# First feed-forward pairs: five k-tiles in two halves and three whole, where all eight were halved, and the lower half's squares summed on VectorE

## The chip, the cores and the metric

One core of a Trainium2 chip runs the whole kernel. The metric is the device time of one execution in microseconds (us). TensorE does the matrix products, VectorE and ScalarE the elementwise work, GpSimd a few additions, SyncE issues the transfers.

## The reference

One layer of an encoder for 512 positions and 1024 channels, in float32. This case concerns the seam between its mixing part and its feed-forward part (`rms_norm` divides each position's row by its root mean square):

```python
h = h + rms_norm(merged @ w_out[i], g_mix_post[i])

hn = rms_norm(h, g_ffn_pre[i])
f_gate, f_up = jnp.split(hn @ w_ffn_in[i], 2, axis=-1)
f = (jax.nn.silu(f_gate) * f_up) @ w_ffn_out[i]
h = h + rms_norm(f, g_ffn_post[i])
```

`w_ffn_in` has 1024 rows and 2 x 2816 columns, so the hidden size is 22 tiles of 128.

## The kernel before

Channels lie on the 128 partitions and positions along the free axis, so an activation of 1024 channels is eight tiles ("k-tiles") of 128 x 512. The positions are also taken in two halves of 256, `lo_half` and `hi_half`. For precision each product is made of three matmuls (`mm3`): both operands are split into a high and a low part, and high x high, high x low and low x high are accumulated in one PSUM bank. Splitting is a cast on ScalarE and a subtraction on VectorE.

`Residual.tile(k)` makes one k-tile of the new `h` for one half: VectorE multiplies the mixed output `o_all` by the inverse root mean square `o_inv` and adds it to `h_all`, ScalarE writes the scaled high part `hg[k][:, 0]`, and VectorE, one step later (`flush`), the low part `hg[k][:, 1]`. The feed-forward product uses `hg`, that is `h` with its gain but without its own root mean square; that factor, `h_inv`, is multiplied in afterwards, in `swiglu`, position by position. It needs the sum of squares of all eight tiles, `h_sums`: ScalarE squares (`square_h`), and `add_h` adds up. `inv_rms` then sums over partitions with a matmul into `ps_stat` and runs `rsqrt`, eight dependent VectorE instructions.

The first three gate and up pairs of the feed-forward product (six banks, six weight blocks) are made with the k-tile in the outer loop (`product_k_outer`), so that TensorE can start as soon as the first k-tiles of the lower half are there: `STAT_A` = 2 k-tiles of the lower half come ahead of the matmul for `o_inv` of the upper half, the other six behind it, and then the upper half's eight, with the matmul for `h_inv` ahead of the last one (`STAT_H` = 7). The lower half's squares are added on GpSimd, the upper half's on VectorE between the residual's steps. Inside `with order():` every engine keeps the order in which the code is written. There are 7 PSUM banks for such products: six are held by the three pairs, the seventh takes `ffn_tile(0)`, and `ffn_tile(1)` needs the first bank that `swiglu` has read.

Of the kernel before, what the change touches and what calls it, by code (L numbers as in the profile page):

```python
# [20 lines left out]
KT = D // P  # L21
# [10 lines left out]
FULL = slice(0, T)  # L32
# [18 lines left out]

DMA_K = 5
STAT_K, STAT_A, STAT_H, STAT_F = 3, 2, 7, 2
MIX_CUT = ((), (0,), (1, 2), (3, 4, 5, 6, 7))
PLE_CUT = (1, 2, 3, 4, 5, 6, 8)
PLE_SPLIT = 3
# [29 lines left out]
def hybrid_block(  # L86
# [7 lines left out]
    nc = tc.nc  # L94
    order = InOrder(tc)
    dve, act_e, pe = order.engine(nc.vector), order.engine(nc.scalar), order.engine(nc.tensor)
# [9 lines left out]
    def bank(name):  # L106
        return psum.tile([P, T], F32, tag="ps", name=name)

    def wide_tile(name):
        return wide.tile([P, KT, T], F32, tag="wide", name=name)  # L110

    def slot(tag, name, dt=F32R, shape=(2, T)):
        return act.tile([P, *shape], dt, tag=tag, name=name, bufs=6 if tag == "tm" else 8)

    def t2(name, n=T):
        return tmp.tile([P, n], F32, tag="t2", name=name)

    def row(name):
        return stat.tile([P, T], F32, tag="row", name=name)
# [99 lines left out]
    def mm3(out, wh, wl, xh, xl, first, last):  # L219
        pe.matmul(out, lhsT=wh, rhs=xh, start=first, stop=False)  # L220
        pe.matmul(out, lhsT=wh, rhs=xl, start=False, stop=False)
        pe.matmul(out, lhsT=wl, rhs=xh, start=False, stop=last)

    def blk(w, k):
        return w[:, k * P:(k + 1) * P]
# [5 lines left out]
            mm3(ps[:, hs], blk(hi, i), blk(lo, i), a[:, 0, hs], a[:, 1, hs],  # L231
                k0 + i == 0, last and i == len(acts) - 1)

    def product_k_outer(banks, blocks, acts, hs, ks=range(KT)):
        for k in ks:
            a = acts[k]
            for ps, (hi, lo) in zip(banks, blocks):
                mm3(ps[:, hs], blk(hi, k), blk(lo, k), a[:, 0, hs], a[:, 1, hs],
                    k == 0, k == len(acts) - 1)


    background = []
# [29 lines left out]
    def inv_rms(sums, y):  # L272

        rsqrt(y, channel_mean(sums), t2("rs_t", sums.shape[1]))
# [13 lines left out]
    def add_sq(sums, sq, i, engine):  # L288
        if i == 1:
            dve.scalar_tensor_tensor(out=sums, in0=sq, scalar=EPS * D / P, in1=sums,  # L290
                                     op0=ALU.add, op1=ALU.add)
        else:
            engine.tensor_tensor(out=sums, in0=sums, in1=sq, op=ALU.add)
# [134 lines left out]
    banks = [bank("ps_first") for _ in range(2 * N_RAW)]  # L428
# [310 lines left out]
    o_all = wide_tile("o_all")  # L739
# [26 lines left out]
    hg = [slot("cv", f"hg{k}") for k in range(KT)]  # L766
    o_sums = row("o_sums")
    h_sums = row("h_sums")
    h_inv = row("h_inv")

    def mix_tile(n, w, hs):
        ps = bank("ps_o")
        product(ps, w, mix_T, hs)
        act_e.activation(out=o_all[:, n, hs], in_=ps[:, hs], func=AF.Copy, scale=col("g_mix_post", n))
        if n == 0:
            act_e.activation(out=o_sums[:, hs], in_=ps[:, hs], func=AF.Square)
            return None
        return square(ps[:, hs], "o_sq")

    def add_mixed(sq, n, hs):  # L780
        if n:
            add_sq(o_sums[:, hs], sq, n, dve)
# [4 lines left out]
    def square_h(k, hs):  # L787
        sq = o_all[:, k, hs] if k else h_sums[:, hs]
        act_e.activation(out=sq, in_=h_all[:, k, hs], func=AF.Square)

    def add_h(k, hs, engine):
        if k:
            add_sq(h_sums[:, hs], o_all[:, k, hs], k, engine)

    lo_half, hi_half = HALVES
    with order():
        for n in range(KT - N_HALF):
            sq = mix_tile(n, weights.get(2), FULL)
            add_mixed(sq, n, FULL)
            weights.ahead((5, 7, 9, 10)[n])  # L800
        late = [weights.get(0) for _ in range(N_HALF)]
        blocks = [weights.get(0) for _ in range(2 * N_PAIR)]
        for i in range(N_HALF):
            n = KT - N_HALF + i
            add_mixed(mix_tile(n, late[i], lo_half), n, lo_half)
        sqs = []
        for i in range(N_HALF):
            n = KT - N_HALF + i
            sq = mix_tile(n, late[i], hi_half)
            if i == 0:  # L810
                y = t2("o_inv", H)
                inv_rms(o_sums[:, lo_half], y)
                res = Residual(o_all, lo_half, y, hg, ffn_gain)
            sqs.append((sq, n))
            for k in MIX_CUT[i]:
                res.tile(k)
                if sqs:
                    add_mixed(*sqs.pop(0), hi_half)
        res.flush()


        banks = [bank("ps_f") for _ in range(2 * N_PAIR)]
        product_k_outer(banks, blocks, hg, lo_half, range(STAT_A))
        for k in range(KT):
            square_h(k, lo_half)
            add_h(k, lo_half, nc.gpsimd)
        y = t2("o_inv", H)
        inv_rms(o_sums[:, hi_half], y)
        res = Residual(o_all, hi_half, y, hg, ffn_gain)
        for k in range(KT):  # L830
            res.tile(k)
            if k > 1:
                add_h(k - 2, hi_half, dve)
            if k:
                square_h(k - 1, hi_half)
        res.flush()
        square_h(KT - 1, hi_half)
        add_h(KT - 2, hi_half, dve)
        add_h(KT - 1, hi_half, dve)
        weights.ahead(2)  # L840
        product_k_outer(banks, blocks, hg, lo_half, range(STAT_A, KT))
        product_k_outer(banks, blocks, hg, hi_half, range(STAT_H))
        inv_rms(h_sums, h_inv)
        product_k_outer(banks, blocks, hg, hi_half, range(STAT_H, KT))

    f_T = []

# [67 lines left out]
    with order():  # L915
# [29 lines left out]
        blocks = [weights.get(0) for _ in range(2)]  # L945
        k = 0
# [9 lines left out]
        banks = [bank("ps_pg") for _ in range(N_LAST)]  # L956
# [82 lines left out]
```

## Time and profile before

| | |
|---|---|
| median of 3 runs | 981.67 us (981.36 to 981.8) |
| the profiled execution's own time | 981.52 us |
| its span, first to last instruction | 979.7 us |
| TensorE busy | 972.2 us (99%) |
| VectorE / ScalarE / GpSimd busy | 672.3 / 350.2 / 83.3 us |
| mean granted TensorE clock | 0.999 |

The profiled execution takes 1.82 us more than its span, and its time is 0.15 us below the median. A busy TensorE is one that always has a matmul under way. How fast they follow one another is read from the starts of successive ones, since they overlap.

### The profile page before, as it was taken

To read this page: it belongs to the slowest core of one execution; us is meant where nothing else is said; L and a number is where in the kernel's file an instruction comes from. 1 tells how busy PE (TensorE), PEld (TensorE's weight loads), DVE (VectorE), ACT (ScalarE), POOL (GpSimd) and SP (SyncE) were. 2 spreads that over 40 slices of the span, in tenths; PEclk is the share of its full clock that TensorE was granted. 3 is DMA by queue.
4 is the path that set the end of the run, shared out by engine and by line. 5 is a ranking of instruction groups with operands and counts; after the bars stand their busy time and mean duration, and the time that the engine had idled before them with its cause. 6 is when DMAs were issued, how large, how long until landed. Compare 5 with 4: busy or idle time off the path is not lost.

```text
span 979.7 us, 11730 instructions
## 1 busy us (share of the span) xinstructions
PE 972.2 (99%) x4683; PEld 818.0 (83%) x4683; DVE 672.3 (69%) x905; ACT 350.2 (36%) x487; POOL 83.3 (9%) x63
## 2 busy tenths in 40 slices
PE   9999999999999999999999999999999999999998
PEld 6888888788888878888888998888888888888897
DVE  6987789999988899967555677544454432223575
ACT  7522323432214432246326433323232322223442
POOL 1100013000013702260000010000000000000000
PEclk9999999999999999999999999999999999999999
DMA  8723322223222322332337112232323233334312
GB/s 305 192 95 100 113 90 73 100 86 101 94 86 91 104 86 89 105 108 86 108 111 274 46 44 79 94 103 90 108 86 104 88 99 98 99 86 139 110 42 86
DMA packets 30726, 102.76 MB, mean 105 GB/s; under 512 B 3536, under 2 KB 4048, under 8 KB 30672
## 3 DMA queue, kind: packets, MB, share of 16 engines
q1 hardware_dynamic: 29808, 99.75, 31.1%
q0 software_dynamic: 720, 2.23, 1.3%
q8 instruction: 36, 0.59, 0.2%
q14 instruction: 18, 0.15, 0.0%
q10 hardware_dynamic: 144, 0.04, 0.0%
HBM read 97.68 MB, written 2.10 MB: 102 GB/s over the span
## 4 chain that ended last, share of the span: by engine, by line
PE 94%; DVE 4%; issue 1%; ACT 0%; DMA 0%; SPq 0%; ACTq 0%
PE ps_f L73 25%; PE ps_br L73 13%; PE ps_fo L73 12%; PE ps_gate L73 12%; PE ps_nat L73 6%; PE ps_ag L73 6%; PE ps_pg L73 5%; PE ps_o L73 5%; PE ps_z L73 4%; PE ps_first L73 3%; DVE lo L73 1%; PE ps_ple L73 1%; PE ps_pool L73 1%; DVE v_all L73 1%; DVE acc L73 1%
## 5 line engine op out<-in xcount | busy, mean ns | idle before, releaser
L73 ACT CAST hi<-raw 128x1024 fp32r<-128x1024 f32 (+1 forms) x157 | 161.6, 1031 | 454.0 <-PE ps_br L73 88.4
L73 DVE TENSOR_TENSOR lo<-raw,hi 128x1024 fp32r<-128x1024 f32 (+2 forms) x155 | 203.9, 1317 | 107.1 <-ACT hi L73 106.6
L73 DVE SCALAR_TENSOR_TENSOR acc<-h_conv,vec,acc 128x511 f32<-128x511 f32 (+14 forms) x240 | 183.3, 764 | 5.2
L73 PE MATMUL ps_f<-hg,hi 128*128 128x512 f32 (+1 forms) x624 | 184.4, 378 | 0.0
L73 PEld LDWEIGHTS ps_f<-hg,hi 128*128 128x128 f32 x624 | 115.1, 188 | 21.7
L73 PE MATMUL ps_gate<-hn,hi 128*128 128x512 f32 x384 | 119.5, 392 | 0.9 <-DVE gated L73 0.9
L73 PE MATMUL ps_f<-hg,lo 128*128 128x512 f32 (+1 forms) x312 | 117.8, 378 | 0.0
L73 PE MATMUL ps_fo<-f,hi 128*128 128x512 f32 (+1 forms) x396 | 110.8, 366 | 0.0
L73 PEld LDWEIGHTS ps_gate<-hn,hi 128*128 128x128 f32 x384 | 71.9, 188 | 17.1 <-DVE gated L73 1.3
L73 PEld LDWEIGHTS ps_fo<-f,hi 128*128 128x128 f32 x396 | 71.7, 189 | 12.1
L73 PE MATMUL ps_nat<-hi,hn 128*128 128x512 f32 x256 | 78.8, 389 | 0.0
L73 PE MATMUL ps_gate<-hn,lo 128*128 128x512 f32 x192 | 74.8, 390 | 0.0
L73 PE MATMUL ps_fo<-f,lo 128*128 128x512 f32 (+1 forms) x198 | 72.4, 365 | 0.0
L73 PEld LDWEIGHTS ps_f<-hg,lo 128*128 128x128 f32 x312 | 58.7, 188 | 11.0
L73 PEld LDWEIGHTS ps_nat<-hi,hn 128*128 128x128 f32 x256 | 48.1, 188 | 10.0
L73 DVE TENSOR_TENSOR f<-ps_f,h_inv 128x512 f32<-128x512 f32 x22 | 15.2, 689 | 56.5 <-PE ps_f L73 56.5
L73 PE MATMUL ps_nat<-lo,hn 128*128 128x512 f32 x128 | 49.8, 389 | 0.0
L73 PE MATMUL ps_ag<-hn,hi 128*128 128x512 f32 x160 | 49.3, 389 | 0.0
L73 PEld LDWEIGHTS ps_fo<-f,lo 128*128 128x128 f32 x198 | 37.3, 189 | 6.1
L73 PEld LDWEIGHTS ps_gate<-hn,lo 128*128 128x128 f32 x192 | 36.0, 188 | 7.5
L73 DVE TENSOR_TENSOR silu<-ps_f,h_inv 128x512 f32<-128x512 f32 x22 | 15.2, 690 | 36.3 <-PE ps_f L73 36.2
L73 PE MATMUL ps_br<-pool,hi 128*128 128x512 f32 x128 | 39.6, 389 | 0.0
(221 smaller groups left out, 1560.2 us busy)
## 6 DMA issues: line engine op xcount, KB each, us to landing
raw<-in_w_mix SPq DMA_DIRECT2D x90, 512.0 KB, 3.3
raw<-in_w_ffn_in SPq DMA_DIRECT2D x44, 512.0 KB, 3.3
raw<-in_w_ffn_out SPq DMA_DIRECT2D x16, 448.0 KB, 3.3
raw<-in_w_ffn_out SPq DMA_DIRECT2D x8, 512.0 KB, 3.6
raw<-in_w_ple_gate SPq DMA_DIRECT2D x8, 512.0 KB, 3.8
x_all<-in_xT SPq DMA_DIRECT2D x8, 256.0 KB, 6.4
h_all<-in_xT SPq DMA_DIRECT2D x4, 512.0 KB, 6.2
out_dram<-pg SPq DMA_DIRECT2D x7, 256.0 KB, 2.0
```

Source lines behind the costliest of these rows:

```text
L73: inst = op(*args, **kw)
```

## The change

In the block that makes the first three pairs, three things differ. The lower half's squares are no longer added on GpSimd as they are made, but on VectorE behind the upper half's. `K_HALF` = 5 k-tiles are still multiplied in halves, the other three at the full width of 512 positions. And since the lower half has started each bank, the upper half's first matmul doesn't clear it (`started`).

```diff
+K_HALF = 5
...
-    def product_k_outer(banks, blocks, acts, hs, ks=range(KT)):
+    def product_k_outer(banks, blocks, acts, hs, ks=range(KT), started=False):
...
-                    k == 0, k == len(acts) - 1)
+                    k == 0 and not started, k == len(acts) - 1)
...
-    def add_h(k, hs, engine):
+    def add_h(k, hs):
         if k:
-            add_sq(h_sums[:, hs], o_all[:, k, hs], k, engine)
+            add_sq(h_sums[:, hs], o_all[:, k, hs], k, dve)
...
         for k in range(KT):
             square_h(k, lo_half)
-            add_h(k, lo_half, nc.gpsimd)
...
         square_h(KT - 1, hi_half)
-        add_h(KT - 2, hi_half, dve)
-        add_h(KT - 1, hi_half, dve)
+        add_h(KT - 2, hi_half)
+        add_h(KT - 1, hi_half)
+        for k in range(KT):
+            add_h(k, lo_half)
         weights.ahead(2)
-        product_k_outer(banks, blocks, hg, lo_half, range(STAT_A, KT))
-        product_k_outer(banks, blocks, hg, hi_half, range(STAT_H))
+        product_k_outer(banks, blocks, hg, lo_half, range(STAT_A, K_HALF))
+
+        product_k_outer(banks, blocks, hg, hi_half, range(K_HALF), started=True)
+        product_k_outer(banks, blocks, hg, FULL, range(K_HALF, STAT_H))
         inv_rms(h_sums, h_inv)
-        product_k_outer(banks, blocks, hg, hi_half, range(STAT_H, KT))
+        product_k_outer(banks, blocks, hg, FULL, range(STAT_H, KT))
```

On TensorE, this is the end of the lower half's k-tile 4 (`hg4`) and what follows it; `ps_f` with a number is a bank, `x2` two matmuls with the same weights. Before:

```order
L73 MATMUL ps_f_4321<-hg4_3847,hi_4036 128x256 x2
L73 MATMUL ps_f_4321<-hg4_3847,lo_4037 128x256
L73 MATMUL ps_f_4316<-hg5_3848,w_hi_3948 128x256 x2
L73 MATMUL ps_f_4316<-hg5_3848,w_lo_3949 128x256
L73 MATMUL ps_f_4317<-hg5_3848,w_hi_3983 128x256 x2
```

The same place in the changed kernel:

```order
L75 MATMUL ps_f_4321<-hg4_3847,hi_4036 128x256 x2
L75 MATMUL ps_f_4321<-hg4_3847,lo_4037 128x256
L75 MATMUL ps_f_4316<-hg0_3843,w_hi_3948 128x256 x2
L75 MATMUL ps_f_4316<-hg0_3843,w_lo_3949 128x256
L75 MATMUL ps_f_4317<-hg0_3843,w_hi_3983 128x256 x2
```

Behind the lower half's k-tile 4 came the lower half's k-tiles 5 to 7; now the upper half's k-tile 0 (`hg0`) comes at once, three k-tiles of half width sooner.

On VectorE, this is the end of the lower half's residual, the `rsqrt` for the upper half's `o_inv`, and the first upper tile (`hg_3843` is k-tile 0, `hg_3850` k-tile 7). Before:

```order
L73 SCALAR_TENSOR_TENSOR hg_3850<-h_all,vec,hg_3850 128x256
L73 SCALAR_TENSOR_TENSOR h_sums<-o_all,h_sums 128x256
L73 TENSOR_SCALAR o_inv<-ps_stat 128x256
...
L73 SCALAR_TENSOR_TENSOR o_inv<-rs_t,o_inv 128x256
L73 TENSOR_TENSOR o_all<-o_all,o_inv 128x256
L73 TENSOR_TENSOR h_all<-h_all,o_all 128x256
L73 TENSOR_TENSOR o_all<-o_all,o_inv 128x256
L73 SCALAR_TENSOR_TENSOR hg_3843<-h_all,vec,hg_3843 128x256
```

In the changed kernel:

```order
L75 SCALAR_TENSOR_TENSOR hg_3850<-h_all,vec,hg_3850 128x256
L75 TENSOR_SCALAR o_inv<-ps_stat 128x256
...
L75 SCALAR_TENSOR_TENSOR o_inv<-rs_t,o_inv 128x256
L75 TENSOR_TENSOR o_all<-o_all,o_inv 128x256
L75 TENSOR_TENSOR h_all<-h_all,o_all 128x256
L75 TENSOR_TENSOR o_all<-o_all,o_inv 128x256
L75 SCALAR_TENSOR_TENSOR hg_3843<-h_all,vec,hg_3843 128x256
```

One addition of squares is gone from between the lower half's last tile and the `rsqrt`; the rest of that chain is as it was.

The last place is VectorE behind the upper half's last tile, ahead of the split of the next two weight blocks (`w_lo`) and of `h_inv`. Before:

```order
L73 SCALAR_TENSOR_TENSOR hg_3850<-h_all,vec,hg_3850 128x256
L73 TENSOR_TENSOR h_sums<-h_sums,o_all 128x256 x2
L73 TENSOR_TENSOR w_lo<-raw,w_hi 128x1024 x2
L73 TENSOR_SCALAR h_inv<-ps_stat 128x512
L73 TENSOR_TENSOR rs_t<-h_inv 128x512
```

In the changed kernel:

```order
L75 SCALAR_TENSOR_TENSOR hg_3850<-h_all,vec,hg_3850 128x256
L75 TENSOR_TENSOR h_sums<-h_sums,o_all 128x256 x2
L75 SCALAR_TENSOR_TENSOR h_sums<-o_all,h_sums 128x256
L75 TENSOR_TENSOR h_sums<-h_sums,o_all 128x256 x6
L75 TENSOR_TENSOR w_lo<-raw,w_hi 128x1024 x2
L75 TENSOR_SCALAR h_inv<-ps_stat 128x512
```

Seven additions now stand between the upper half's sums and the split of the weights.

## Rows read from the trace of the kernel before

**Rows 1.** The page: busy time, share of the span, instructions.

```profile
PE 972.2 (99%) x4683; PEld 818.0 (83%) x4683; DVE 672.3 (69%) x905; ACT 350.2 (36%) x487; POOL 83.3 (9%) x63
```

**Rows 2.** TensorE's waits: for whom, us in total, times, longest.

```profile
PE ps_gate L73 <- DVE gated L73: 0.9, 1, 0.9
```

**Rows 3.** Timeline of TensorE: start, us, operation, count.

```profile
566.23 0.40 PE L73 MATMUL ps_f<-hg,w_hi 128*128 128x256 f32 x2
...
572.71 0.40 PE L73 MATMUL ps_f<-hg,w_hi 128*128 128x256 f32 x2
...
587.83 1.02 PE L73 MATMUL ps_stat<-h_sums,mean_mat 128*128 128x512 f32 x2
...
590.84 0.63 PE L73 MATMUL ps_f<-hg,w_hi 128*128 128x512 f32 x2
...
596.31 0.62 PE L73 MATMUL ps_f<-hg,w_hi 128*128 128x512 f32 x2
...
601.75 0.62 PE L73 MATMUL ps_f<-hg,w_hi 128*128 128x512 f32 x2
```

**Rows 4.** Timeline of VectorE, upper half's `rsqrt` and first tiles.

```profile
562.26 0.48 DVE L73 SCALAR_TENSOR_TENSOR hg<-h_all,vec,hg 128x256 fp32r<-128x256 f32 x1 [0.58 <-ACT hg L73]
...
563.22 0.42 DVE L73 TENSOR_SCALAR o_inv<-ps_stat 128x256 int32<-128x256 int32 x1
563.67 0.82 DVE L73 TENSOR_TENSOR rs_t<-o_inv 128x256 f32<-128x256 f32 x1
...
566.32 0.42 DVE L73 TENSOR_TENSOR rs_t<-rs_t,ps_stat 128x256 f32<-128x256 f32 x1
...
568.99 0.42 DVE L73 TENSOR_TENSOR h_all<-h_all,o_all 128x256 f32<-128x256 f32 x1
...
569.99 0.48 DVE L73 SCALAR_TENSOR_TENSOR hg<-h_all,vec,hg 128x256 fp32r<-128x256 f32 x1 [0.24 <-ACT hg L73]
570.39 0.42 DVE L73 TENSOR_TENSOR h_all<-h_all,o_all 128x256 f32<-128x256 f32 x1
...
571.39 0.48 DVE L73 SCALAR_TENSOR_TENSOR hg<-h_all,vec,hg 128x256 fp32r<-128x256 f32 x1 [0.24 <-ACT hg L73]
```

**Rows 5.** Timeline of GpSimd in the same stretch.

```profile
563.47 2.53 POOL L293 TENSOR_TENSOR h_sums<-h_sums,o_all 128x256 f32<-128x256 f32 x3 [124.82 <-ACT o_all L73]
...
566.08 2.60 POOL L293 TENSOR_TENSOR h_sums<-h_sums,o_all 128x256 f32<-128x256 f32 x3
```

**Rows 6.** Timeline of VectorE, the same chain for the lower half.

```profile
546.58 0.42 DVE L73 TENSOR_SCALAR o_inv<-ps_stat 128x256 int32<-128x256 int32 x1 [2.10 <-PE ps_stat L73]
...
550.71 0.42 DVE L73 TENSOR_TENSOR h_all<-h_all,o_all 128x256 f32<-128x256 f32 x1
```

**Rows 7.** Timeline of TensorE where it resumes after a wait.

```profile
185.72 0.73 PE L73 MATMUL ps_gate<-hn,hi 128*128 128x512 f32 x2 [0.87 <-DVE gated L73]
186.29 0.40 PE L73 MATMUL ps_gate<-hn,lo 128*128 128x512 f32 x1
```

**Rows 8.** Timeline of VectorE behind the upper half's last tile.

```profile
580.20 0.95 DVE L73 TENSOR_TENSOR h_sums<-h_sums,o_all 128x256 f32<-128x256 f32 x2
...
581.35 2.36 DVE L73 TENSOR_TENSOR w_lo<-raw,w_hi 128x1024 fp32r<-128x1024 f32 x2 [0.20 <-ACT w_hi L73]
...
588.89 0.69 DVE L73 TENSOR_SCALAR h_inv<-ps_stat 128x512 int32<-128x512 int32 x1 [5.18 <-PE ps_stat L73]
...
594.76 0.69 DVE L73 TENSOR_TENSOR silu<-ps_f,h_inv 128x512 f32<-128x512 f32 x1
```

**Rows 9.** Timeline of TensorE: the kernel's first and last matmuls.

```profile
1.33 3.81 PE L73 MATMUL ps_warm<-warm_up 128*128 128x512 bf16 x9 [1.33 <-DVE warm_up L73]
...
975.41 0.28 PE L73 MATMUL ps_pg<-h,lo 128*128 128x256 f32 x1
```

**Rows 10.** Windows: length, busy time per engine, granted clock (PEclk), DMA.

```profile
977.80:977.90 0.10, 0.00 (x0) 0.00 (x0) 0.00 (x0) 0.00 (x0) 0.00 (x0) 1.00 0.14 51
...
978.00:978.10 0.10, 0.00 (x0) 0.00 (x0) 0.00 (x0) 0.00 (x0) 0.00 (x0) 0.50 0.97 338
```

More of the change, by code (lines that the diff above doesn't have):

```diff
@@ L832, in hybrid_block @@
             if k > 1:
-                add_h(k - 2, hi_half, dve)
+                add_h(k - 2, hi_half)
             if k:
```

## The prediction, made before the changed kernel ran

> **What bounds the kernel now.** I read the page first. TensorE is busy for 972.2 of 979.7 us [rows 1], so time is lost or won only where TensorE's own work changes or where it has to wait. The list of TensorE's waits comes next: it has five entries, and apart from the start of the kernel the longest is 0.9 us, far from this change [rows 2]. Nothing in the stretch from 559 to 591 us makes TensorE wait today. So the timeline of that stretch decides, and two things in it: how fast matmuls of either width follow one another [rows 3], and when VectorE delivers the upper half's first tile [rows 4]. Today that tile's low part ends at 569.99 + 0.48 = 570.47 us, and TensorE comes to it at 572.71 us [rows 3, 4]: 2.24 us of slack. The change takes three k-tiles of half width out of just that place.
>
> **Wider matmuls.** One k-tile of a half is six banks of three matmuls, 18 in all. From 566.23 to 572.71 us TensorE goes through three of them, 54 matmuls, so one starts every 0.120 us and a k-tile of a half takes 2.16 us. At full width, eight groups of three take 5.44 us from 596.31 to 601.75, that is 0.68 us for three, 0.2267 us each [rows 3]. Three k-tiles are 18 groups of three. In halves they cost 36 x 0.36 = 12.96 us, whole 18 x 0.68 = 12.24 us. The saving is 0.72 us, all of it on TensorE and so on the path. Its bounds: the first eight groups behind this block take 5.47 us [rows 3], which makes it 0.65; nothing in the rows makes it more than 0.72. I take 0.72. The Trainium skill, "TensorE: Matmul & The Clock Gate", section "Back-to-back issue gap", gives columns / 2.4 + 2.5 ns between isolated matmuls, so that two halves would cost only 2.5 ns more than one whole, and the saving would be 54 x 2.5 ns = 0.14 us. The rows say 13.3 ns (2 x 120 - 226.7), and the measurement decides.
>
> **When the upper half's first tile is ready.** Two things go out of VectorE's way. First, the addition of squares between the lower half's last tile and the `rsqrt`: behind such a low part the next independent instruction starts 0.40 us later (569.99 to 570.39), so `o_inv` can start at 562.26 + 0.40 = 562.66 instead of 563.22, 0.56 us sooner [rows 4]. Second, GpSimd's six additions, which run from 563.47 to 568.68 us [rows 5]. In that time four of VectorE's instructions, each with both inputs in SBUF, took 0.82 to 0.85 us (the first is at 563.67), while those of the same size that read `ps_stat` kept to 0.42 [rows 4]. From `o_inv` to the first `h_all` the upper half takes 568.99 - 563.22 = 5.77 us [rows 4]; the same nine steps for the lower half, with GpSimd idle, take 550.71 - 546.58 = 4.13 us [rows 6]. That is 1.64 us sooner. Both together are 2.20 us: the first low part ends at 570.47 - 2.20 = 568.27 us.
>
> **When TensorE wants it.** With the lower half's k-tiles 5 to 7 gone from this place, it comes to the upper half's k-tile 0 at 566.23 us, where k-tile 5 began [rows 3]. The first matmul of the tile takes the high part; the second, due at 566.23 + 0.12 = 566.35, takes the low part, and the whole queue stands behind it. It waits until 568.27: 1.92 us. Resuming costs a little more: behind the wait at 185.72 us the first two matmuls took 0.57 us (to 186.29) where two take 0.45 (2 x 0.2267) [rows 7], so 0.11 on top. The stall is 2.03 us. Below, it could lack the 0.11; above, if nothing of the 1.64 came, it would be 3.67.
>
> No second stall follows: VectorE delivers a tile every 1.40 us (569.99 to 571.39) [rows 4], TensorE uses one in 2.16. The second is ready at 569.67, and TensorE is there at 568.27 + 0.11 + 17 x 0.12 = 570.42. Later ones have more room, and the three full-width k-tiles come when both halves have long been there.
>
> **The seven additions that move.** They stand on VectorE behind the upper half's sums, which end at 580.20 + 0.95 = 581.15 today [rows 8] and at 578.95 with the 2.20 us gained. At up to 0.53 us apiece (the pair in that row ends 0.95 us after it began, 0.42 of it the last one) seven take up to 3.7 us, to 582.7. Behind them wait the two splits of weight blocks, 2.36 us [rows 8], to about 585.3, and behind those `h_inv`. TensorE reaches the matmul for `h_inv` at 570.42 + 4 x 2.16 + 12 x 0.68 = 587.22 us, against 587.83 now [rows 3]. VectorE sits idle for 5.18 us ahead of `h_inv` today [rows 8]; the additions use some 3.7 of it, less the 2.20 gained. They cost nothing, with about 2 us to spare. If that cover were gone, each us would delay `h_inv`. The transfers that refill the split blocks' buffers start about 1.5 us later than now; the blocks they bring are wanted only by tiles beyond `ffn_tile(1)`, after 601 us.
>
> Next behind `h_inv` is its eight-step `rsqrt` and the first bank that `swiglu` frees, at 594.76 + 0.69 = 595.45 us; `ffn_tile(1)` wants it at 596.31 [rows 3, 8]. This slack of 0.86 us grows: `h_inv` comes 0.61 us sooner, TensorE comes to `ffn_tile(1)` later. The matmul for `h_inv` is followed by a full k-tile, 4.08 us, instead of 2.16, so `ffn_tile(0)` starts 1.92 - 0.61 = 1.31 us later than its 590.84 [rows 3]. From there to the end the list of waits has nothing longer than the entry of [rows 2], so a shift passes through to the end.
>
> **The sum.** + 2.03 (stall) + 0 (additions moved, transfers, `h_inv`) - 0.72 (wider matmuls) = + 1.31 us. The span goes from 979.7 to 981.0 and the profiled execution from 981.52 to 982.83; the median stands 0.15 above that one, so I predict 983.0 us, 0.13% slower. A difference of 0.2%, about 2 us, is what a measurement of this kernel can tell from no change, so this counts as the same. The forecast's own range is 982.4 to 983.6.
>
> **Rivals.**
>
> *TensorE's clock falls in the stall.* Its mean over the span is 0.999 of 2.4 GHz, so the wait of 0.9 us [rows 2] did not lower it. But at the end of the kernel, where the last matmul ends at 975.69 us, the clock is still 1.00 at 977.9 and 0.50 (1.2 GHz) at 978.0 us [rows 9, 10]: 2.3 us of idleness were enough there. This stall is 0.3 us shorter, with one matmul in it. What a fall would cost is bounded by the kernel's first matmuls: eight and a half times 512 columns took 3.81 us, 0.448 each [rows 9], against 0.2267, so 1.9 us were lost until the rate rose. With the stall that is + 3.2 us, 984.9, slower by 0.33%. It decides from the point at which the idleness lowers the clock, and a fall in some executions only would move the median only if it were most of them. Chance 0.12.
>
> *GpSimd is not what slows VectorE's four instructions.* Then only 0.56 us are gained, the stall is 3.67 us, and the sum + 2.95: 984.6 us, slower by 0.30%. Against it is the lower half's chain [rows 6]. The Trainium skill, "SBUF — State Buffer", section "Who interferes with whom", says that a VectorE instruction with two inputs in SBUF contends with a GpSimd one that reads SBUF, and that one with a single such input does not; the rows agree, 0.82 against 0.42. Chance 0.04.
>
> *There is no stall to speak of.* If the tile came two microseconds sooner than I work out, only the saving would be left: - 0.72 us, 980.95, 0.07% faster, which counts as the same. For it speaks that the chain would be free of GpSimd; against it, that its eleven dependent steps up to the low part are all in the rows, and 4.13 us of them [rows 6] cannot begin before 562.66. Chance 0.08.
>
> *The additions delay `h_inv`.* They would need more than 2 us over their rows to make the matmul for `h_inv` late, and then also hold TensorE, since the next k-tile stands behind it. Each further us is a us; 1 us more gives 984.0, slower by just over 0.2%. Chance 0.05.
>
> **How the numbers follow.** The forecast has 0.69; with the no-stall case 0.77. The two ends of unknown costs that are slower by over 0.2% (clock, GpSimd, additions) have 0.21. For faster by over 0.2% I find no mechanism and leave 0.02. So faster 0.02, same 0.77, slower 0.21. The range reaches down over the better part of the forecast's lower side, 982.0, and up to the clock and GpSimd cases, 984.9.
>
> **What will show it.** In the changed kernel's profile, a wait of TensorE for `hg` of about 2 us in `ps_f` (a stall near 566.4 us, ended by VectorE's low part near 568.3); no VectorE instruction of 256 columns above 0.5 us between 562 and 569; 0.227 us between matmuls in the last three k-tiles; the matmul for `h_inv` near 587.2 and `h_inv` directly behind it; `ffn_tile(0)` near 592.2. The prediction is wrong if the wait is under 1 us or over 3, if the clock is below 1.00 behind it, or if another wait of TensorE appears behind 570.

## The result and the profile after

The changed kernel takes 984.43 us (median of 10 executions, 983.07 to 985.28), the kernel before 981.8 us (10 executions, 981.36 to 982.34): a ratio of 1.0025, 95% interval 1.0017 to 1.0033 (the ratios in this document aren't those of the two medians, from which they differ by up to 0.0004). That is 2.6 us or 0.25% slower, inside the predicted range of 982.0 to 984.9 but outside the forecast's own 982.4 to 983.6, and 1.4 us above the predicted 983.0. The profiled execution took 984.39 us, with a span of 982.6 us against 979.7.

The list of TensorE's waits in the changed kernel has one entry that was not there before (for whom, us in total, times, longest); the second row answers to [rows 2]:

```profile
PE ps_f L75 <- ACT hg L75: 1.4, 1, 1.4
...
PE ps_gate L75 <- DVE gated L75: 0.9, 1, 0.9
```

VectorE's timeline over the upper half's `rsqrt` and first tiles in the changed kernel, which answers to [rows 4]:

```profile
562.26 0.49 DVE L75 SCALAR_TENSOR_TENSOR hg<-h_all,vec,hg 128x256 fp32r<-128x256 f32 x1 [0.58 <-ACT hg L75]
562.66 0.41 DVE L75 TENSOR_SCALAR o_inv<-ps_stat 128x256 int32<-128x256 int32 x1
563.11 0.42 DVE L75 TENSOR_TENSOR rs_t<-o_inv 128x256 f32<-128x256 f32 x1
...
566.78 0.42 DVE L75 TENSOR_TENSOR h_all<-h_all,o_all 128x256 f32<-128x256 f32 x1
...
567.78 0.48 DVE L75 SCALAR_TENSOR_TENSOR hg<-h_all,vec,hg 128x256 fp32r<-128x256 f32 x1 [0.24 <-ACT hg L75]
...
569.17 0.48 DVE L75 SCALAR_TENSOR_TENSOR hg<-h_all,vec,hg 128x256 fp32r<-128x256 f32 x1 [0.24 <-ACT hg L75]
```

`o_inv` starts at 562.66 us, none of the nine steps behind it takes more than 0.43, and the first low part ends at 567.78 + 0.48 = 568.26 us. The prediction had 562.66 and 568.27.

TensorE's timeline in the changed kernel, which answers to [rows 3]:

```profile
566.11 0.28 PE L75 MATMUL ps_f<-hg,lo 128*128 128x256 f32 x1
567.80 0.91 PE L75 MATMUL ps_f<-hg,w_hi 128*128 128x256 f32 x2 [1.41 <-ACT hg L75]
568.54 0.28 PE L75 MATMUL ps_f<-hg,w_lo 128*128 128x256 f32 x1
...
569.81 0.41 PE L75 MATMUL ps_f<-hg,w_lo 128*128 128x256 f32 x1
570.03 0.63 PE L75 MATMUL ps_f<-hg,hi 128*128 128x256 f32 x2
570.45 0.41 PE L75 MATMUL ps_f<-hg,lo 128*128 128x256 f32 x1
...
573.02 0.40 PE L75 MATMUL ps_f<-hg,w_hi 128*128 128x256 f32 x2
573.26 0.28 PE L75 MATMUL ps_f<-hg,w_lo 128*128 128x256 f32 x1
...
580.58 0.63 PE L75 MATMUL ps_f<-hg,w_hi 128*128 128x512 f32 x2
...
588.78 1.02 PE L75 MATMUL ps_stat<-h_sums,mean_mat 128*128 128x512 f32 x2
...
593.74 0.62 PE L75 MATMUL ps_f<-hg,w_hi 128*128 128x512 f32 x2
```

The wait is split: the tile's first matmul starts at 567.80 when ScalarE has written the high part, the second (merged into the same row) stands until VectorE's low part, and the third comes at 568.54, where 566.47 was its time. That is the stall of 2.07 us; the prediction had 2.03. But from 569.39 to 572.59 two matmuls with the same weights and a third with others take 0.64 us (569.81 to 570.45) instead of 0.36. The windows of the changed kernel say why (length; busy us of TensorE, its weight loads, VectorE, ScalarE, GpSimd; granted clock; DMA):

```profile
566.00:568.00 2.00, 0.59 (x5) 0.37 (x3) 1.69 (x5) 0.51 (x1) 0.00 (x0) 1.00 0.00 0
568.00:569.00 1.00, 0.86 (x6) 0.68 (x6) 0.94 (x3) 0.37 (x1) 0.00 (x0) 1.00 0.00 0
569.00:570.00 1.00, 1.00 (x8) 1.00 (x7) 0.82 (x3) 0.45 (x2) 0.00 (x0) 0.67 0.00 0
570.00:571.00 1.00, 1.00 (x7) 1.00 (x6) 0.76 (x3) 0.82 (x2) 0.00 (x0) 0.50 0.00 0
...
572.00:573.00 1.00, 1.00 (x7) 1.00 (x7) 1.00 (x4) 0.41 (x2) 0.00 (x0) 0.62 0.00 0
573.00:574.00 1.00, 1.00 (x11) 1.00 (x10) 1.00 (x4) 0.65 (x2) 0.00 (x0) 1.00 0.00 0
```

The clock is 1.00 (2.4 GHz) during the wait and for almost a microsecond behind it, falls to 0.50 (1.2 GHz) near 569.3, and is back near 572.8. TensorE comes to the first full-width k-tile at 580.58 us; the prediction's sum puts that at 570.42 + 4 x 2.16 = 579.06. The difference is 1.52 us: 0.04 of it is the longer stall, and 1.48 is what the fall cost. From there all goes nearly as predicted: the matmul for `h_inv` comes 8.20 us later (predicted 8.16), `ffn_tile(0)` starts at 593.74, 2.90 us later than before, and the span is 2.9 us longer. Stall and fall add up to 3.55 us, so the wider matmuls gave back 0.65 of the predicted 0.72.

The clock seems to have fallen in most executions, not in all; only one of them was profiled, for the others there are the mean clock and the time. Of the ten, seven have a mean clock of 0.998 and take 984.26 to 985.28 us; three have 0.999 or 1.000 and take 983.07, 983.27 and 983.54.

The seven additions, in VectorE's timeline of the changed kernel, answer to [rows 8]:

```profile
577.98 0.95 DVE L75 TENSOR_TENSOR h_sums<-h_sums,o_all 128x256 f32<-128x256 f32 x2
...
579.30 2.73 DVE L75 TENSOR_TENSOR h_sums<-h_sums,o_all 128x256 f32<-128x256 f32 x6
581.95 2.35 DVE L75 TENSOR_TENSOR w_lo<-raw,w_hi 128x1024 fp32r<-128x1024 f32 x2
589.84 0.69 DVE L75 TENSOR_SCALAR h_inv<-ps_stat 128x512 int32<-128x512 int32 x1 [5.54 <-PE ps_stat L75]
```

They end at 582.03, the weight splits at 584.30, and VectorE then waits 5.54 us for TensorE: the additions delay nothing.

### The profile page after: what moved, and what is told of

It is laid out like the page before. It is cut to its first block, busy times and chain, and to the rows that moved or that the text cites. A ratio compares the mean times of both kernels' runs of the same rounds, so it can differ in the third digit from the quotient of the medians.

```text
span 982.6 us, 11613 instructions
## 1 busy us (share of the span) xinstructions
PE 973.7 (99%) x4629; PEld 817.0 (83%) x4629; DVE 673.4 (69%) x911; ACT 350.3 (36%) x487; POOL 78.5 (8%) x57
## 4 chain that ended last, share of the span: by engine, by line
PE 91%; DVE 6%; issue 1%; ACT 1%; ACTq 0%
PE ps_f L75 24%; PE ps_br L75 13%; PE ps_fo L75 12%; PE ps_gate L75 12%; PE ps_ag L75 6%; PE ps_pg L75 5%; PE ps_o L75 5%; PE ps_z L75 4%; PE ps_nat L75 4%; PE ps_first L75 3%; DVE lo L75 2%; DVE acc L75 2%; PE ps_ple L75 1%; PE ps_pool L75 1%; DVE v_all L75 1%
## 5 line engine op out<-in xcount | busy, mean ns | idle before, releaser
L75 PE MATMUL ps_f<-hg,w_hi 128*128 128x256 f32 (+1 forms) x152 | 38.8, 344 | 1.5 <-ACT hg L75 1.4
```

Of the source, the lines that this page charges most:

```text
L75: inst = op(*args, **kw)
```

## The experiments

The theory after the result has two parts. The upper half's first tile is ready 1.9 us after TensorE wants it, which costs 2.0 us less the 0.7 that wider matmuls save; and the idleness lowers TensorE's clock in most executions, which costs up to 1.5 us more. Rivals are that the moved additions cost time, that the stall doesn't follow the place in the order, and that the clock falls for another reason. Each run is compared with runs of the kernel before on its own chip: 981.7 us (27 executions) for the additions alone, six k-tiles, the additions on GpSimd and 14 unread matmuls, and 981.59 us (20) for 8 and 4 unread matmuls and four k-tiles.

### The additions alone

Only the second edit: the lower half's squares go to VectorE, all k-tiles stay halved.

```diff
-        product_k_outer(banks, blocks, hg, hi_half, range(K_HALF), started=True)
-        product_k_outer(banks, blocks, hg, FULL, range(K_HALF, STAT_H))
+        product_k_outer(banks, blocks, hg, hi_half, range(STAT_H))
         inv_rms(h_sums, h_inv)
-        product_k_outer(banks, blocks, hg, FULL, range(STAT_H, KT))
+        product_k_outer(banks, blocks, hg, hi_half, range(STAT_H, KT))
```

with `K_HALF = 8`.

> All eight k-tiles stay halved; only the lower half's additions move from GpSimd to VectorE. Theory (stall plus clock): the upper half's first low part ends near 568.3 us as in the changed kernel, but TensorE comes to it only at 572.7, so nothing waits, the clock stays at 1.00 and the time is that of the kernel before, within 0.3 us. Rival (the seven additions on VectorE cost time by themselves, by delaying h_inv): 1 us or more above the kernel before, with a wait of TensorE or a later h_inv behind 580 us.

Measured: 981.5 us (981.39 to 982.65), ratio 1.0002 (0.9993 to 1.0010). VectorE's timeline of this kernel:

```profile
567.94 0.48 DVE L75 SCALAR_TENSOR_TENSOR hg<-h_all,vec,hg 128x256 fp32r<-128x256 f32 x1 [0.24 <-ACT hg L75]
```

The low part is as early as in the changed kernel (568.4 against 570.5 before), and it is worth nothing as long as TensorE comes to it only at 572.9 in this run. The additions cost nothing either. The first rival falls.

### Six k-tiles in halves

`K_HALF = 6` in the changed kernel, nothing else.

> Six k-tiles in halves, two whole, everything else as in the changed kernel. Theory: TensorE comes to the upper half's first low part at 568.5 us, just behind its end at 568.3, so there is no stall and no fall of the clock, and two k-tiles save 2 x 0.24 us: 0.5 us faster than before (981.3), with little spread from execution to execution. Rival (the stall comes from somewhere else than the place in the order, or full-width tiles lower the clock): as the changed kernel, 1 to 3 us slower than before.

Measured: 981.34 us (980.96 to 981.88), ratio 0.9997 (0.9988 to 1.0006). TensorE's timeline of this kernel where the upper half begins:

```profile
568.45 0.28 PE L75 MATMUL ps_f<-hg,lo 128*128 128x256 f32 x1
568.57 0.40 PE L75 MATMUL ps_f<-hg,w_hi 128*128 128x256 f32 x2
568.81 0.28 PE L75 MATMUL ps_f<-hg,w_lo 128*128 128x256 f32 x1
...
590.60 0.61 PE L75 MATMUL ps_f<-hg,w_hi 128*128 128x512 f32 x2
```

The pace of 0.12 us goes on without a wait, and the list of waits has no entry for `ps_f`. So the stall follows the place in the order. The medians differ by 0.36 us in the expected direction; the interval doesn't tell that from nothing. The trace does: from the upper half's k-tile 0 to `ffn_tile(0)` TensorE takes 22.03 us (568.57 to 590.60). Before, it took 18.13 (572.71 to 590.84 [rows 3]), and the lower half's last two k-tiles ahead of that 4.32. So 0.42 us are saved, of the expected 0.48.

### Five and three, with the additions on GpSimd

```diff
         for k in range(KT):
             square_h(k, lo_half)
+            add_h(k, lo_half, nc.gpsimd)
...
-        for k in range(KT):
-            add_h(k, lo_half)
```

(`add_h` takes the engine as an argument again.)

> The five and three k-tiles of the changed kernel, but the lower half's additions left on GpSimd. Theory (GpSimd slows VectorE's chain by 1.64 us, the additions' place costs 0.56): the low part ends at 570.5 instead of 568.3, the stall is 4.2 us, and the time is 3.5 us above the kernel before at full clock, 4 to 5.5 with the clock's fall. Rival (the second edit matters only for the sums): the same 2 to 3 us above as the changed kernel.

Measured: 986.73 us (986.60 to 987.68), ratio 1.0053 (1.0041 to 1.0066): 5.0 us over the kernel before. VectorE's timeline of this kernel:

```profile
562.67 0.48 DVE L75 SCALAR_TENSOR_TENSOR hg<-h_all,vec,hg 128x256 fp32r<-128x256 f32 x1 [0.58 <-ACT hg L75]
...
563.63 0.42 DVE L75 TENSOR_SCALAR o_inv<-ps_stat 128x256 int32<-128x256 int32 x1
564.08 0.83 DVE L75 TENSOR_TENSOR rs_t<-o_inv 128x256 f32<-128x256 f32 x1
564.94 0.42 DVE L75 SCALAR_TENSOR_TENSOR rs_t<-rs_t,ps_stat 128x256 f32<-128x256 f32 x1
565.40 0.42 DVE L75 SCALAR_TENSOR_TENSOR o_inv<-rs_t,o_inv 128x256 f32<-128x256 f32 x1
...
569.38 0.42 DVE L75 TENSOR_TENSOR h_all<-h_all,o_all 128x256 f32<-128x256 f32 x1
...
570.38 0.48 DVE L75 SCALAR_TENSOR_TENSOR hg<-h_all,vec,hg 128x256 fp32r<-128x256 f32 x1 [0.24 <-ACT hg L75]
```

and TensorE's:

```profile
566.53 0.28 PE L75 MATMUL ps_f<-hg,lo 128*128 128x256 f32 x1
570.40 1.10 PE L75 MATMUL ps_f<-hg,w_hi 128*128 128x256 f32 x2 [3.59 <-ACT hg L75]
```

With GpSimd adding, four instructions take 0.83 to 0.85 us again, the ones that read `ps_stat` 0.42, and TensorE's wait is 3.59 us instead of 1.41: 2.18 us more, the predicted 2.20. The timeline shows its two parts. `o_inv` starts 0.96 us after the start of the last low part instead of 0.40, and from there to the first `h_all` it takes 5.75 us instead of 4.12. But two more instructions with both inputs in SBUF keep to 0.42 while GpSimd adds, those at 565.40 and 567.19, as their counterparts at 564.98 and 566.78 did in the kernel before. So GpSimd's additions slow four of six such instructions here; why not the other two is open. The second edit is what keeps the first one from costing 5 us.

### The wait filled with matmuls that nobody reads

In three kernels TensorE is given matmuls of 256 columns on the zero warm-up tile where it waits, 14, 8 or 4 of them, into the bank that `ps_stat` also uses. They change nothing of the output.

```diff
         product_k_outer(banks, blocks, hg, lo_half, range(STAT_A, K_HALF))
-
+        ps_idle = psum.tile([P, T], F32, tag="pst", name="ps_idle", bufs=1)
+        for _ in range(14):
+            pe.matmul(ps_idle[:, :H], lhsT=warm_up[:, :P], rhs=warm_up[:, :H], start=True, stop=True)
         product_k_outer(banks, blocks, hg, hi_half, range(K_HALF), started=True)
```

> The changed kernel with 14 matmuls of 256 columns on the zero warm-up tile, into a bank that nobody reads, where TensorE waits for the upper half's first tile. Theory (the clock falls because TensorE idles there): the matmuls fill 1.7 to 1.9 us of the stall, the clock stays at 1.00 in every execution, and the time is 1.2 to 1.5 us above the kernel before (983.0) with a spread of less than 1 us. Rival (the clock falls for another reason, or the spread has another source): a median near 984.4 and a spread of 2 us, as the changed kernel, or more by what the added matmuls take.

> The changed kernel with 8 of the unread matmuls where TensorE waits. They take 0.9 us, so TensorE idles for about 1.0 us. Theory (the length of the idleness decides on the clock, and 0.9 us elsewhere in this kernel doesn't lower it): no fall, 983.0 to 983.3, spread under 1 us. Rival (any wait at this place lowers it): median near 984.4 and a spread of 2 us.

> The changed kernel with 4 of the unread matmuls, which take 0.5 us: TensorE idles for about 1.4 us instead of 1.9. Theory: a fall in fewer executions than the changed kernel's eight in ten, so a median between 983.1 and 984.4. If there is none, the idleness that lowers the clock lies between 1.4 and 1.9 us here; if as many, below 1.4.

| unread matmuls | TensorE's wait for `hg` in the profile | median us (range, executions) | ratio to before |
|---|---|---|---|
| 0 (the changed kernel) | 1.41 | 984.43 (983.07 to 985.28, 10) | 1.0025 (1.0017 to 1.0033) |
| 4 | 0.95 | 983.12 (982.66 to 983.92, 11) | 1.0015 (1.0006 to 1.0024) |
| 8 | 0.52 | 983.20 (982.77 to 983.79, 11) | 1.0016 (1.0007 to 1.0025) |
| 14 | none | 983.29 (982.65 to 983.78, 11) | 1.0015 (1.0006 to 1.0025) |

TensorE's timeline with 4 of them:

```profile
566.16 0.61 PE L75 MATMUL ps_idle<-warm_up 128*128 128x256 bf16 x4
567.72 0.91 PE L75 MATMUL ps_f<-hg,w_hi 128*128 128x256 f32 x2 [0.95 <-ACT hg L75]
...
592.17 0.62 PE L75 MATMUL ps_f<-hg,w_hi 128*128 128x512 f32 x2
```

and a window of the same kernel behind the wait:

```profile
569.00:573.00 4.00, 4.00 (x35) 4.00 (x35) 3.66 (x11) 2.25 (x7) 0.00 (x0) 1.00 0.02 4
```

The stall itself is left as it was, since the tile comes no sooner: all three stand 1.5 to 1.6 us over the kernel before, near the predicted 1.3. In the trace with 4 of them, TensorE takes 26.01 us from this place to `ffn_tile(0)` (566.16 to 592.17), against 24.61 before (566.23 to 590.84 [rows 3]): 1.40 us of stall less saving, without a fall. In the changed kernel it is 2.90. But the clock stays at 1.00 in the three profiles and at 0.999 or 1.000 on average in every execution, none is above 983.92, and the median is 1.1 to 1.3 us below the changed kernel's. So TensorE's idleness lowers the clock, and half a microsecond less of it was enough to avoid that in all of 11 executions. With 4 I had expected some falls, fewer than the changed kernel's (seven in ten, not the eight that I wrote); there were none. The spreads, 1.0 to 1.3 us, are a little more than the 1 us below which I expected those of 8 and 14; the kernel before spreads by 1.3 us beside 14 and by 0.7 beside the others.

### Four k-tiles in halves

`K_HALF = 4` in the changed kernel, nothing else.

> Four k-tiles in halves, four whole, otherwise the changed kernel. Theory: TensorE comes to the upper half's first low part at 564.2 us and waits until 568.3, 4.1 us and 0.1 to resume, less 4 x 0.24 saved: 3.2 us above the kernel before at full clock, and since the idleness is twice that of the changed kernel the clock falls in every execution, for 1.5 us more: 986.4. Rival (the loss per k-tile taken out is a fixed price, not the data's time): twice the changed kernel's 2.6 less nothing, or the same 984.4 as the changed kernel.

Measured: 986.48 us (986.42 to 987.99), ratio 1.0049 (1.0035 to 1.0063). TensorE's timeline of this kernel, and then its windows:

```profile
564.63 0.28 PE L75 MATMUL ps_f<-hg,lo 128*128 128x256 f32 x1
568.48 1.10 PE L75 MATMUL ps_f<-hg,w_hi 128*128 128x256 f32 x2 [3.57 <-ACT hg L75]
```

```profile
566.00:567.00 1.00, 0.00 (x0) 0.00 (x0) 0.90 (x4) 0.00 (x0) 0.00 (x0) 1.00 0.00 0
567.00:568.00 1.00, 0.00 (x0) 0.00 (x0) 0.96 (x3) 0.08 (x1) 0.00 (x0) 0.92 0.00 0
...
573.00:574.00 1.00, 1.00 (x6) 1.00 (x6) 1.00 (x4) 0.49 (x2) 0.00 (x0) 0.50 0.00 0
574.00:576.00 2.00, 2.00 (x16) 2.00 (x15) 2.00 (x7) 1.15 (x4) 0.00 (x0) 0.83 0.00 0
```

The wait is 2.16 us longer than with five, exactly the one k-tile that was taken out, so the loss follows the data's time and is no fixed price. All five executions are above 986.4, and with 3.59 us of waiting in the experiment with GpSimd all five are at 986.6 or above; the mean clock is 0.996 to 0.998 in all ten. These ten were measured together with the filled kernels, so the clock could still fall when those were run. In the profiled one, 987.99 us, the clock falls while TensorE still waits and stays down until after 574; the other four lie within 0.07 us of one another, 1.6 to 1.7 us over the 3.2 at full clock.

## Why the prediction was right, and in which step it was not

**The stall.** Right in mechanism and size. The low part was predicted to end at 568.27 and ends at 568.26; the stall was to be 2.03 us and is 2.07, since resuming took 0.16 instead of 0.11. Its place is shown by six and by four k-tiles in halves. What shortens it, the one addition less (predicted 0.56) and GpSimd idle (1.64), is 0.56 and 1.63 in the timeline of the experiment that puts the additions back. GpSimd was right as the cause, though not every VectorE instruction with both inputs in SBUF is slowed.

**Wider matmuls.** Right, at the lower of the two bounds: the first two full-width k-tiles take 8.20 us where 8.16 were worked out, and in all 0.65 us were saved instead of 0.72. By the formula that the Trainium skill, "TensorE: Matmul & The Clock Gate", section "Back-to-back issue gap", gives for isolated matmuls, the halves would have cost only 2.5 ns more per pair than the wholes, an estimate. The rows of the changed kernel give 0.120 us and 0.227 to 0.228 us, 12 to 13 ns a pair, so that formula doesn't hold for this dense stream.

**The additions, the transfers, `h_inv`.** Nothing was to be late, and nothing is: alone they give 981.5 against 981.7.

**The sum without the clock.** The forecast's 983.0 fits, within 0.5 us, the three executions of the changed kernel whose mean clock is that of the kernel before (983.07 to 983.54) and, within 0.3, the three kernels with the wait filled (983.1 to 983.3).

**The clock.** This is the step that failed. The rival was named, with its place, but given a chance of 0.12, on the ground that this stall is 0.3 us shorter than the idleness at the kernel's end behind which the clock fell, with one matmul in it. That row was taken for a bound, and it was only one instance. The clock fell in seven of ten executions, so the median is that of a kernel whose clock falls, and the prediction's own sign of being wrong, a clock below 1.00 behind the stall, is there. That the time still lies in the range is because the range had been drawn up to this rival's 984.9. The rival's price was too high as well: 1.9 us from the kernel's first matmuls, against 1.48 in the profile and some 1.2 in the median. The rows of the kernel before (a timeline, and a window: length, TensorE busy, granted clock, DMA) don't bear that price out:

```profile
1.33 3.81 PE L73 MATMUL ps_warm<-warm_up 128*128 128x512 bf16 x9 [1.33 <-DVE warm_up L73]
4.98 3.22 PE L73 MATMUL ps_first<-xg,first 128*128 128x512 f32 x11
```

```profile
1.30:5.20 3.90, 3.87 (x10) 1.00 0.75 227
```

From start to start the nine matmuls take 3.65 us, 1.6 more than nine at 0.2267; the "eight and a half" of the prediction stands in no row, and with a granted clock of 1.00 in the row the profile doesn't show that the clock was what slowed them. So the time comes to 984.4 instead of 983.0, and "the same within 0.2%", to which 0.77 was given, was missed by 0.05%.

## What to carry to other kernels

Work that is made narrower or earlier, so that it can start before all its data is there, is also cover. Before it is taken out, find when the next operand is ready and when the engine would come to it; here 2.24 us of slack were there, 2.20 were gained, and 6.5 were taken. Price the idleness of TensorE by more than its length: here a wait of 1.4 us brought matmuls at half pace behind it in most executions, one of 0.95 us in none, and a few matmuls on dead data avoided that, though not the wait. GpSimd additions that are off the path can still slow VectorE steps that are on it; here four of nine took twice as long.

## What was not expected of the hardware

In the profiled execution of the changed kernel the clock doesn't fall while TensorE waits, but 0.9 us after it has resumed: idle from 566.4 to 567.8, one matmul, idle again until 568.4, then full, and down from 569.3 to 572.8 us. At 1.2 GHz, 256 columns took 0.213 us instead of 0.120, so the loss in those 3.4 us was 1.5 and not half of them. With longer waits the fall comes earlier: while TensorE still waits with four k-tiles in halves, and near 570.3, just before it resumes at 570.40, in the experiment with GpSimd, whose windows are these:

```profile
570.00:571.00 1.00, 0.60 (x2) 0.37 (x2) 0.76 (x3) 0.35 (x1) 0.00 (x0) 0.63 0.00 0
571.00:572.00 1.00, 1.00 (x5) 1.00 (x6) 0.76 (x3) 0.77 (x2) 0.00 (x0) 0.50 0.00 0
```

By mean clock and time, the changed kernel's clock fell in seven executions of ten and not in the other three; the kernels with waits of 0.95 and 0.52 us had it fall in none of 22. Why the executions differ was not settled.
